# Both streams' h side by side in one tile, their shared products 512 columns wide, and the gate logits kept in DRAM until the merge

## The chip, the cores and the metric

The kernel runs on one core of a Trainium2 chip. The metric is the device time of one execution in microseconds. Engines are named as in the profile: PE is TensorE's matmuls and PEld its weight loads, DVE the vector engine, ACT the scalar engine, POOL GpSimd, SP SyncE, which issues most of the DMAs.

## What is computed

One layer over a latent stream x (256 tokens) and a context stream ctx (256 tokens), D = 2048, all in float32. Both streams are modulated and projected; only the latent stream goes on to an output. Cut to what matters here:

```python
mod, mod_c = silu(c) @ w_mod + b_mod, silu(c_ctx) @ w_mod + b_mod
h  = modulate(rmsnorm(x,   norm_g[0]), sh_a,  sc_a)
hc = modulate(rmsnorm(ctx, norm_g[0]), csh_a, csc_a)
# p = h @ w_in, split into c_q, c_kv, k_r, hg_q, hg_ff, hg_fb, hg_i, hg_g, gate_logits (for h and for hc)
attn_l = block_attention(q_l, concat([k_c, k_l]), concat([v_c, v_l]))      # 8 heads, latent queries
hgo_c, s_f, s_b = hgrn2_bidirectional(*hg_c[:6], zero, zero)               # 8 heads, context first,
hgo_l, _, _     = hgrn2_bidirectional(*hg_l[:6], s_f, s_b)                 # then latent from its states
g = sigmoid(gate_logits_l)                                                 # (256, 2, 2048)
out_l = (g[0] * (attn_l @ w_br_mla) + g[1] * ((rmsnorm(hgo_l) * silu(hgate)) @ w_br_hgrn)) @ w_out
x = x + gt_a * rmsnorm(out_l, norm_g[1])
h = modulate(rmsnorm(x, norm_g[2]), sh_f, sc_f)
x = x + gt_f * rmsnorm(swiglu(h, w_ffn_in, w_ffn_out), norm_g[3])
```

## The kernel before

**Arithmetic.** Channels lie on the 128 partitions and tokens on the columns. Every float32 operand of a product is split into a rounded high part and the rest, weights as wH and wL (`split_w`, the cast on ACT at line 100, the subtraction on DVE at line 102), activations as a pair (aH, aL). A product is wH·aH + wH·aL + wL·aH. K = 2048 is 16 slices of 128, k = 0 to 15. `mm3` (lines 116 to 125) writes these three products for each of the streams that it is given, all 256 columns wide: six matmuls per k for both streams (H·aH and H·aL of the first, of the second, then L·aH of each), three for one. `mm_wide` (lines 127 to 130) does one stream in two matmuls: the pair [aH | aL] side by side, 512 columns, with wH, then 256 columns with wL; the two halves of the result are added later.

**Order.** The kernel is written in program order, and a scheduler sets each engine's order from that, from the buffers of the pools and from modelled times. The pools are wp (three each of raw, wH, wL), ap (16 each of hA, hB; 8 of hC), bp (two of 32 KB per partition, tag b16) and two of PSUM, pj and px, four banks each. Weights come as raw tiles of 1 MB on SP's queue (`load_w`); the weights of the first six blocks (wst, tile rw) come on POOL's queue.

**Stages.**
- Startup, 0 to 143 us. 32 weight tiles for the modulation pass through PE (pm, line 256). As soon as a group of one or two k is modulated, `make_h` (lines 191 to 199) makes h of both streams for them, on DVE (195), ACT (196) and DVE (197), into one tile hA (latent) and one hB (context), each [aH | aL]. `pre_mm` then adds this k to the first six projection blocks (NPRE = 6, PSUM tiles pre).
- Latents and heads, to 555 us. `project` (lines 326 to 334) does one block of 128 output channels: 16 k's of `mm3` into one PSUM bank ps, the latent stream in columns 0 to 255, the context stream in 256 to 511. Eight heads (`hgrn_head`) have five blocks each; value and both forget gates are for both streams, query and output gate for the latent stream alone. While PE does one head's blocks, DVE and ACT do the gate chains (the scans that make the decays), and PE takes in the small products of the head before: transposes pk of the keys kt (line 471, copied to ktn at 474), chunk products pc (479).
- Gates and attention, to 827 us. `gates` (569 to 581) makes the 32 blocks of gate logits with `mm_wide`, 16 k's each; ACT copies one half out of PSUM, DVE adds the other, into a tile sgt (128 x 512, for both branches of one j) that takes the slot of an hB. The tiles pe of the softmax come from the hB slots as well. Attention is written between the gate blocks; its pk at line 125 has three 512-column matmuls per k, psS at 656 has three of 512 columns with 64 rows.
- Merge, to 919 us (lines 705 to 723). For each j of 16, 48 matmuls psb (line 713); sigmoid of sgt on ACT (715), multiplication by psb on DVE (716), the sum m of both branches on POOL (718), then the split into mg, which takes the slot of an hA.
- Output projection (`project_tok`, pst, line 778), norm, feed-forward, to the end. It reuses hA and hB slots for the split weights of the last tiles, h2 and G, and `gate_rows` (736 to 750) makes the second norm's gate vectors.

Of the kernel before, what the change touches and what calls it, by code (L numbers as in the profile page):

```python
# [14 lines left out]
P = 128  # L15
T = 256
# [10 lines left out]
def block_kernel(  # L27
# [83 lines left out]

    def split_act(dst, src, heng=None):
        nc.scalar.copy(dst[:, 0, :], src)
        nc.vector.tensor_tensor(dst[:, 1, :], src, dst[:, 0, :].bitcast(F32), op=ALU.subtract)
# [57 lines left out]
    hs = [[None] * KD, [None] * KD]  # L172
# [18 lines left out]
    def make_h(k):  # L191
        for s, tag in ((0, "hA"), (1, "hB")):
            h = ap.tile([P, 2, T], F32R, tag=tag, name=tag)
# [5 lines left out]
            hs[s][k] = h  # L199
# [126 lines left out]
    def project(nb, streams):  # L326
# [239 lines left out]
    aT = bp.tile([P, NH, 2, T], F32R, tag="b16", name="aT")  # L566
    sgt = []

    def gates(b):

        if b % 2 == 0:
            sgt.append(ap.tile([P, 512], F32, tag="hB", name="sgt"))
# [3 lines left out]
        for k in range(KD):  # L576
            mm_wide(ps, w(k * P, P), hs[0][k], k == 0, k == KD - 1)
# [66 lines left out]
    def att_s(i, A):  # L644
# [4 lines left out]
        for qb in range(2):  # L649
# [10 lines left out]
            pe = ap.tile([P, 512], F32, tag="hB", name="pe")  # L660
# [44 lines left out]
    mg = []  # L705
    for j in range(KD):
        w = split_w(load_w(wbr[j]))
# [28 lines left out]
    def gate_rows(i, tag, bufs):  # L736
# [8 lines left out]
        tiles = []  # L745
        for c in range(4):
            g = ap.tile([P, 512], F32, tag=tag, name="gbc", bufs=bufs)
            nc.sync.dma_start(g, gdr[i, 4 * c:4 * c + 4].rearrange("k p -> (k p)").partition_broadcast(P))
            tiles.append(g)
        return tiles  # L750

    def project_tok(tiles, nk, src, first, last, lead=None):
# [6 lines left out]
        for q in range(nq):  # L759
            raw = load_w(tiles(q))  # L760
            if lead and q == nq - 1:
                ws.append(split_w(raw, step=512, tags=(lead[0], lead[0]), pool=ap, bufs=lead[1]))
# [31 lines left out]
    g1b = gate_rows(0, "hC", 8)  # L794
# [281 lines left out]
```

## Time and profile before

| | us |
|---|---|
| median of 3 runs | 1767.45 (1766.27 to 1767.64) |
| profiled execution | 1768.12 |
| its span in the trace | 1766.3 |
| PE busy | 1725.0 |
| DVE busy | 1110.0 |
| ACT busy | 800.1 |
| startup, to the last group's products | 0 to 143 |
| latents and heads | 143 to 555 |
| gates and attention | 555 to 827 |
| merge | 827 to 919 |

The rows of the trace follow after the change. Busy time counts the records of an engine; matmuls are pipelined and their records overlap, so what a matmul costs in a stream is read from the distance between starts. The chain that ended last is followed back from the last instruction, at each step to what released it. In rows on stretches of time the columns are: start and end of the stretch, its length, then for PE, PEld, DVE, ACT and POOL the busy us and in brackets the number of instructions, then the TensorE clock that was granted as a share of 2.4 GHz, the mean busy share of the 16 DMA engines, and GB/s. In timelines, "x4" is a run of four instructions, and brackets give the idle time before and what ended it.

### The profile page before, as it was taken

Reading aid. Unit: us, or ns where it says so; the run is one execution under the profiler, and the core shown is the slowest. Engines: PE = TensorE matmul, PEld = TensorE weight load, DVE = VectorE, ACT = ScalarE, POOL = GpSimd, SP = SyncE. Lnnn points to the kernel's source line nnn. Section 1 sums busy time; section 2 is a strip of 40 time slices with the busy share of each in tenths; the row PEclk is TensorE's granted clock in tenths of the full one; section 3 lists DMA queues with packets and bytes.
Section 4 is the critical chain, followed back from the end, with each engine's and each line's share of the span. In section 5 each row is a group of like instructions: output and inputs, shape, how many; then the busy total and the mean of one; then the engine's idle time right before and its main releaser. Section 6 shows DMA issues by size and latency. Waiting matters only on the chain.

```text
span 1766.3 us, 26819 instructions
## 1 busy us (share of the span) xinstructions
PE 1725.0 (98%) x10976; PEld 1528.4 (87%) x10976; DVE 1110.0 (63%) x1703; ACT 800.1 (45%) x1178; POOL 38.6 (2%) x57
## 2 busy tenths in 40 slices
PE   4999999999999999999999899999999999999998
PEld 2779999999999888888998698888888888888886
DVE  4335777766678766666775687776445555555556
ACT  4224433333334655555444554444444444334443
POOL 2100000000000000000110000000000000000000
PEclk9999999999999999999999999999999999999999
DMA  9985456555556555566765457777555555555563
GB/s 361 331 320 194 140 178 208 191 191 170 175 173 231 212 182 207 177 248 232 260 228 200 169 178 275 281 276 257 195 192 185 188 191 190 192 191 189 181 215 130
DMA packets 56459, 374.64 MB, mean 212 GB/s; under 512 B 6512, under 2 KB 6800, under 8 KB 13072
## 3 DMA queue, kind: packets, MB, share of 16 engines
q1 hardware_dynamic: 53424, 365.06, 59.1%
q0 software_dynamic: 2048, 6.29, 1.1%
q8 instruction: 86, 1.41, 0.3%
q10 hardware_dynamic: 864, 1.57, 0.2%
q14 instruction: 37, 0.30, 0.0%
HBM read 370.79 MB, written 2.11 MB: 211 GB/s over the span
## 4 chain that ended last, share of the span: by engine, by line
PE 97%; DVE 1%; DMA 1%; ACT 1%; issue 0%; SPq 0%; DVEq 0%; ACTq 0%
PE ps L125 20%; PE pst L778 18%; PE psf L129 18%; PE psf L130 9%; PE ps L129 7%; PE psb L713 5%; PE pre L125 4%; PE ps L130 3%; PE pm L256 2%; PE psf L872 1%; PE psS L656 1%; PE po L679 1%; PE psS L653 1%; DMA xt<-in_xT_dram 1%; PE pv L628 1%; PE pq L612 1%
## 5 line engine op out<-in xcount | busy, mean ns | idle before, releaser
L102 DVE TENSOR_TENSOR wL<-raw,wH 128x1024 fp32r<-128x1024 f32 (+1 forms) x492 | 597.5, 1217 | 462.4 <-ACT wH L100 461.3
L100 ACT CAST wH<-raw 128x1024 fp32r<-128x1024 f32 (+1 forms) x492 | 508.7, 1037 | 748.7 <-PE ps L125 182.1
L129 PE MATMUL psf<-h,wH 128*128 128x512 f32 x1344 | 475.1, 399 | 0.0
L130 PE MATMUL psf<-h,wL 128*128 128x256 f32 x1344 | 377.5, 281 | 0.0
L129 PEld LDWEIGHTS psf<-h,wH 128*128 128x128 f32 x1344 | 252.6, 188 | 62.8
L125 PE MATMUL ps<-hA,wH 128*128 128x256 f32 x1312 | 254.6, 285 | 0.0
L130 PEld LDWEIGHTS psf<-h,wL 128*128 128x128 f32 x1344 | 253.9, 189 | 0.2
L125 PEld LDWEIGHTS ps<-hA,wH 128*128 128x128 f32 x1312 | 204.8, 192 | 1.2 <-issue 0.5
L125 PE MATMUL ps<-hA,wL 128*128 128x256 f32 x656 | 187.3, 286 | 0.0
L129 PE MATMUL ps<-hA,wH 128*128 128x512 f32 x512 | 183.8, 400 | 0.0
L778 PE MATMUL pst<-wH,gA 128*128 128x512 f32 x576 | 166.6, 389 | 0.0
L321 DVE CUSTOM_DVE_ANT_0 raw<-raw,cb 128x2048 f32<-128x2048 f32 x64 | 146.0, 2281 | 29.9 <-DMA raw<-in_wm_dram 29.7
L130 PE MATMUL ps<-hA,wL 128*128 128x256 f32 x512 | 144.0, 282 | 0.0
L125 PE MATMUL ps<-hB,wH 128*128 128x256 f32 x672 | 137.2, 284 | 0.0
L778 PEld LDWEIGHTS pst<-wH,gA 128*128 128x128 f32 x576 | 108.0, 188 | 22.3
L125 PEld LDWEIGHTS ps<-hA,wL 128*128 128x128 f32 x656 | 125.7, 192 | 0.5 <-issue 0.5
L129 PEld LDWEIGHTS ps<-hA,wH 128*128 128x128 f32 x512 | 96.0, 188 | 22.9 <-issue 1.3
L125 PEld LDWEIGHTS ps<-hB,wH 128*128 128x128 f32 x672 | 105.0, 192 | 0.0
L778 PE MATMUL pst<-wL,gA 128*128 128x512 f32 x288 | 101.4, 389 | 0.0
L130 PEld LDWEIGHTS ps<-hA,wL 128*128 128x128 f32 x512 | 96.5, 189 | 2.6 <-DVE mx L658 1.1
L125 PE MATMUL ps<-hB,wL 128*128 128x256 f32 x336 | 95.2, 283 | 0.0
L778 PE MATMUL pst<-wH,mg 128*128 128x512 f32 x256 | 74.4, 389 | 0.0
(432 smaller groups left out, 2189.3 us busy)
## 6 DMA issues: line engine op xcount, KB each, us to landing
raw<-in_wm_dram SPq DMA_DIRECT2D x96, 1024.0 KB, 5.0
raw<-in_wfi_dram SPq DMA_DIRECT2D x84, 1024.0 KB, 4.9
raw<-in_win_dram SPq DMA_DIRECT2D x73, 1024.0 KB, 4.9
raw<-in_wfo_dram SPq DMA_DIRECT2D x44, 1024.0 KB, 4.8
raw<-in_wbr_dram SPq DMA_DIRECT2D x16, 1024.0 KB, 5.0
raw<-in_wout_dram SPq DMA_DIRECT2D x16, 1024.0 KB, 4.9
rw<-in_wst_dram POOLq DMA_DIRECT2D x16, 256.0 KB, 5.8
raw<-in_wqk_dram SPq DMA_DIRECT2D x4, 1024.0 KB, 4.9
```

The source lines that it names most:

```text
L100: nc.scalar.copy(H, raw[:, o:o + n])
L102: nc.vector.tensor_tensor(L, raw[:, o:o + n], H.bitcast(F32), op=ALU.subtract)
L125: nc.tensor.matmul(o, l, r, start=(first and i == 0), stop=(last and i == len(seq) - 1))
L129: nc.tensor.matmul(ps, w[0], act.rearrange("p e t -> p (e t)"), start=first, stop=False)
L130: nc.tensor.matmul(ps[:, 0:T], w[1], act[:, 0, :], start=False, stop=last)
L256: nc.tensor.matmul(pm[32 * (k % 4):32 * (k % 4) + 32, 0:n], cst[:, k], raw[:, kk * n:(kk + 1) * n], start=(k < 4), stop=(k >= KD - 4))
L321: nc.vector.tensor_tensor_reduce(out=raw, in0=raw, in1=cbt[0], scale=1.0, scalar=0.0, op0=ALU.mult, op1=ALU.add, accum_out=mod2[:, i // KD ...
L612: nc.tensor.matmul(pq[:, i * T:(i + 1) * T], l, r, start=(k == 0 and i == 0 and z == 0), stop=(k == 3 and i == 1 and z == 2))
L628: nc.tensor.matmul(pv[:, i, :], ckvs[:, k, l, ts_], r, start=(i == 0 and k == 0 and z == 0), stop=(i == 1 and k == 1 and z == 2))
L653: nc.tensor.matmul(psS, qn[a][:, i * T + qb * P:i * T + (qb + 1) * P], kn[b], start=(n == 0), stop=False)
L713: nc.tensor.matmul(ps[:, br * T:(br + 1) * T], l, r, start=(br == 0 and k == 0 and z == 0), stop=(br == 1 and k == NH - 1 and z == 2))
L778: mm = nc.tensor.matmul(ps[hf], l, r, start=(k == 0 and n == 0), stop=(k == nk - 1 and n == 2))
```

## The change

1. One tile hx in place of the 32 tiles hA and hB: partition x stream x k x part (high, low) x token. `both(k, 0)` is aH of both streams for one k, `both(k, 1)` is aL: two runs of 256 columns that lie apart in the tile. `pre_mm` and `project` give `mm3` one 512-column output for both streams, so that it writes three matmuls of 512 columns per k (now line 136) in place of six of 256. A block for one stream is as before.
2. Gate logits no longer stay on the chip: `gates` makes them in four places of a tile sgx (slots 0 to 3) and stores each j to DRAM (sgd, line 608); the merge loads them back (line 739) into eight places, four of which held the softmax's pe (slots 4 to 7). Both on POOL's queue. The sigmoid is now line 748, m is line 751.
3. Places in hx that have become free are given out by hand: the attention's output aT, the merged units mg, later h2 (`units`), the split weights of two tiles (`split_into`) and G (`spare`). The second norm's gate vectors go into the place of the modulation's operand (tag cst).

```diff
+    def split_into(raw, tiles):
+        for i, (H, L) in enumerate(tiles):
+            nc.scalar.copy(H, raw[:, i * 512:(i + 1) * 512])
+            nc.vector.tensor_tensor(L, raw[:, i * 512:(i + 1) * 512], H.bitcast(F32), op=ALU.subtract)
...
-    hs = [[None] * KD, [None] * KD]
+    hx = cp.tile([P, 2, KD, 2, T], F32R, name="hx")
+
+    def both(k, e):
+        return hx[:, :, k, e, :]
...
     def make_h(k):
-        for s, tag in ((0, "hA"), (1, "hB")):
-            h = ap.tile([P, 2, T], F32R, tag=tag, name=tag)
+        for s in range(2):
+            h = hx[:, s, k]
...
     def pre_mm(ws, k, b):
-        mm3([pre[b][:, 0:T], pre[b][:, T:2 * T]], ws(b * P, P),
-            [(hs[s][k][:, 0, :], hs[s][k][:, 1, :]) for s in range(2)], k == 0, k == KD - 1)
+        mm3([pre[b].rearrange("p (s t) -> p s t", s=2)], ws(b * P, P), [(both(k, 0), both(k, 1))],
+            k == 0, k == KD - 1)
...
-        outs = [ps[:, s * T:(s + 1) * T] for s in streams]
         for k in range(KD):
-            mm3(outs, w(k * P, P), [(hs[s][k][:, 0, :], hs[s][k][:, 1, :]) for s in streams], k == 0, k == KD - 1)
+            if len(streams) == 2:
+                o, act = ps.rearrange("p (s t) -> p s t", s=2), (both(k, 0), both(k, 1))
+            else:
+                o, act = ps[:, 0:T], (hx[:, 0, k, 0, :], hx[:, 0, k, 1, :])
+            mm3([o], w(k * P, P), [act], k == 0, k == KD - 1)
...
-    aT = bp.tile([P, NH, 2, T], F32R, tag="b16", name="aT")
-    sgt = []
+    aT = hx[:, 1, 0:NH]
+    sgx = bp.tile([P, 8, 512], F32, tag="b16", name="sgx")
+    sgd = dp.tile([KD, P, 512], F32, name="sgd")
+    n_pe = [0]
...
     def gates(b):
+        j = b // 2
...
-        half = sgt[-1][:, (b % 2) * T:(b % 2 + 1) * T]
+        half = sgx[:, j % 4, (b % 2) * T:(b % 2 + 1) * T]
         nc.scalar.copy(half, ps[:, 0:T])
         nc.vector.tensor_tensor(half, half, ps[:, T:2 * T], op=ALU.add)
+        if b % 2 == 1:
+            nc.gpsimd.dma_start(sgd[j], sgx[:, j % 4, :])
         step()
...
-            pe = ap.tile([P, 512], F32, tag="hB", name="pe")
+            pe = sgx[:, 4 + n_pe[0] % 4, :]
+            n_pe[0] += 1
...
+    units = [hx[:, 1, 8 + j] for j in range(8)] + [hx[:, 0, j] for j in range(8)]
+    spare = [hx[:, 1, j] for j in range(8)] + [hx[:, 0, 8 + j] for j in range(8)]
     for j in range(KD):
+        sg = sgx[:, (4 + j) % 8, :]
+        nc.gpsimd.dma_start(sg, sgd[j])
...
-        nc.scalar.activation(sgt[j], sgt[j], AF.Sigmoid)
-        nc.vector.tensor_tensor(sgt[j], ps, sgt[j], op=ALU.mult)
+        nc.scalar.activation(sg, sg, AF.Sigmoid)
+        nc.vector.tensor_tensor(sg, ps, sg, op=ALU.mult)
         m = wk.tile([P, T], F32, tag="hf", name="m", bufs=2)
-        nc.gpsimd.tensor_tensor(m, sgt[j][:, 0:T], sgt[j][:, T:2 * T], op=ALU.add)
-        dst = ap.tile([P, 2, T], F32R, tag="hA", name="mg")
+        nc.gpsimd.tensor_tensor(m, sg[:, 0:T], sg[:, T:2 * T], op=ALU.add)
+        dst = units[j]
...
-            h = ap.tile([P, 2, T], F32R, tag="hB", name="h2")
+            h = units[j]
...
-            g = ap.tile([P, 2, T], F32R, tag="hA", name="gA")
+            g = spare[n_g[0] % 16]
...
-            g2b = gate_rows(1, "hB", 16)
+            g2t = cp.tile([P, 4, 512], F32, tag="cst", name="g2t")
+            g2b = gate_rows(1, [g2t[:, c] for c in range(4)])
```

What this does to the engines' orders is shown at three places, the last of them (the handover of the gate logits) for two engines. A row is line, operation, output <- inputs, shape of the output and a count.

PE at the start of the first six blocks, before: pt and pm belong to the modulation, the pre tiles are the six blocks, hA is the latent stream's h of k = 0, and each block has H·aH first, then H·aL.

```order
L269 MATMUL pt<-c_84,row 128x2 x2
L125 MATMUL pre_95<-hA,wH 128x256
L125 MATMUL pre_96<-hA,wH 128x256
L125 MATMUL pre_97<-hA,wH 128x256
L125 MATMUL pre_98<-hA,wH 128x256
L125 MATMUL pre_95<-hA,wH 128x256
L125 MATMUL pre_96<-hA,wH 128x256
L125 MATMUL pre_97<-hA,wH 128x256
L125 MATMUL pre_98<-hA,wH 128x256
L256 MATMUL pm<-raw,cst 32x256 x16
```

The same place after the change, with ptok and pbc from the second stream's norm:

```order
L289 MATMUL pt<-c_84,row 128x2 x2
L276 MATMUL pm<-raw,cst 32x256 x16
L289 MATMUL pt<-c_84,row 128x2 x2
L154 MATMUL ptok<-ones,acc 128x1 x4
L166 MATMUL pbc<-dg,ones 128x128
L276 MATMUL pm<-raw,cst 32x512 x4
L166 MATMUL pbc<-dg,ones 128x128
L276 MATMUL pm<-raw,cst 32x512 x4
L136 MATMUL pre_96<-hx,wH 128x512
```

The first eight narrow products, which needed the latent stream alone, have left their place ahead of the sixteen pm; the first wide one stands behind the second stream's norm.

PE in the heads around the transposes pk of one pair of chunks, before:

```order
L125 MATMUL ps<-hA,wL 128x256
L125 MATMUL ps<-hB,wL 128x256
L125 MATMUL ps<-hA,wH 128x256 x2
L125 MATMUL ps<-hB,wH 128x256 x2
L471 MATMUL pk<-c_84,kt 128x128 x4
L479 MATMUL pc<-qd_2800,kt 128x128 x2
L125 MATMUL ps<-hA,wL 128x256
L125 MATMUL ps<-hB,wL 128x256
L125 MATMUL ps<-hA,wH 128x256 x2
L125 MATMUL ps<-hB,wH 128x256 x2
```

And after the change:

```order
L136 MATMUL ps<-hx,wH 128x512 x2
L136 MATMUL ps<-hx,wL 128x512
L136 MATMUL ps<-hx,wH 128x512
L494 MATMUL pk<-c_84,kt 128x128 x4
L502 MATMUL pc<-qd_2241,kt 128x128 x2
L136 MATMUL ps<-hx,wH 128x512
L136 MATMUL ps<-hx,wL 128x512
L136 MATMUL ps<-hx,wH 128x512 x2
L136 MATMUL ps<-hx,wL 128x512
```

Three wide rows stand where six narrow ones stood, and pk and pc come between the products as before.

POOL from the startup's last weight load on, before: the two memsets belong to the heads, m to the merge.

```order
L224 DMA rw<-in_wst_dram 128x512
L224 DMA rw<-in_wst_dram 128x256
L387 MEMSET hgx 128x512
L388 MEMSET hgx 128x1600
L718 ISA
L718 TENSOR_TENSOR m<-sgt 128x256 x16
```

And after the change:

```order
L410 MEMSET hgx 128x512
L411 MEMSET hgx 128x1600
L608 DMA sgd<-sgx 128x512 x13
L739 DMA sgx<-sgd 128x512 x3
L608 DMA sgd<-sgx 128x512
L739 DMA sgx<-sgd 128x512 x3
L608 DMA sgd<-sgx 128x512
L739 DMA sgx<-sgd 128x512
L608 DMA sgd<-sgx 128x512
L739 DMA sgx<-sgd 128x512
L751 ISA
L751 TENSOR_TENSOR m<-sgx 128x256
```

The merge's first eight loads have moved in between the last gate logits' stores, ahead of the first m, and from there on a load and an m alternate.

ACT where the sigmoids begin, before: L579 is the copy of a gate block, L715 the sigmoid, L474 belongs to the heads.

```order
L579 COPY sgt<-ps 128x256
L100 CAST wH<-raw 128x1024
L715 ACTIVATE sgt<-sgt 128x512
L474 COPY ktn<-pk 128x512
L100 CAST wH<-raw 128x512
L579 COPY sgt<-ps 128x256
L100 CAST wH<-raw 128x1024
```

And ACT at the handover from the gates to the merge, after the change: L605 is the copy of a gate block, L703 and L711 are attention, L124 is the high part of an activation, L748 the sigmoid of the logits that have come back.

```order
L605 COPY sgx<-ps 128x256
L703 COPY pT_7009<-pp 128x128 x2
L748 ACTIVATE sgx<-sgx 128x512
L703 COPY pT_7011<-pp 128x128 x2
L100 CAST wH<-raw 128x1024 x2
L605 COPY sgx<-ps 128x256
L748 ACTIVATE sgx<-sgx 128x512 x2
L711 COPY of<-po_7078 128x256
L124 CAST hx<-of 128x256
L100 CAST wH<-raw 128x1024 x2
L605 COPY sgx<-ps 128x256
L748 ACTIVATE sgx<-sgx 128x512
```

The sigmoids (L748) of j = 3, of j = 4 and 5 and of j = 6 stand between copies of the last three gate blocks and behind them, each with casts of weights behind it; those of j = 0 to 2 stand some rows higher. Before, the sigmoid of j = 0 followed on the copy of its own gate block, with no transfer between.

## Rows read from the trace of the kernel before

**Rows 1.** The page's busy time: us, share of the span and instructions per engine.
```profile
PE 1725.0 (98%) x10976; PEld 1528.4 (87%) x10976; DVE 1110.0 (63%) x1703; ACT 800.1 (45%) x1178; POOL 38.6 (2%) x57
```

**Rows 2.** The page's chain that ended last, by engine and by line.
```profile
PE 97%; DVE 1%; DMA 1%; ACT 1%; issue 0%; SPq 0%; DVEq 0%; ACTq 0%
PE ps L125 20%; PE pst L778 18%; PE psf L129 18%; PE psf L130 9%; PE ps L129 7%; PE psb L713 5%; PE pre L125 4%; PE ps L130 3%; PE pm L256 2%; PE psf L872 1%; PE psS L656 1%; PE po L679 1%; PE psS L653 1%; DMA xt<-in_xT_dram 1%; PE pv L628 1%; PE pq L612 1%
```

**Rows 3.** Stages: span, busy us (instructions) by engine, PEclk, DMA share, GB/s.
```profile
143.00:555.00 412.00, 412.00 (x3409) 409.89 (x3410) 292.58 (x581) 159.54 (x216) 1.90 (x2) 1.00 0.53 180
555.00:827.00 272.00, 272.00 (x1571) 232.13 (x1570) 185.17 (x297) 155.24 (x255) 0.00 (x0) 1.00 0.59 209
```

**Rows 4.** Waits, 143 to 555 us: engine, line, released by: us, times, longest.
```profile
ACT wH L100 <- PE ps L125: 182.1, 58, 5.6
```

**Rows 5.** Groups of PE by shape: xcount | busy us, mean ns | idle.
```profile
L125 PE MATMUL ps<-hB,wH 128*128 128x256 f32 x672 | 137.2, 284 | 0.0
...
L125 PE MATMUL ps<-hB,wL 128*128 128x256 f32 x336 | 95.2, 283 | 0.0
...
L125 PE MATMUL pre<-hB,wL 128*128 128x256 f32 x96 | 27.4, 286 | 0.0
```

**Rows 6.** Chain in order of time: start us, us, what.
```profile
277.64 21.35 PE ps L125 x178
...
328.97 21.35 PE ps L125 x178
...
717.50 0.90 PE psS L656 x3
...
1224.34 87.06 PE pst L778 x384
```

**Rows 7.** PE's timeline from 597 us: start us, us, what.
```profile
597.47 0.61 PE L125 MATMUL pk<-cqkv,wH 128*128 128x512 f32 x2
...
598.60 0.28 PE L130 MATMUL ps<-hA,wL 128*128 128x256 f32 x1
598.71 0.40 PE L129 MATMUL ps<-hA,wH 128*128 128x512 f32 x1
598.95 0.28 PE L130 MATMUL ps<-hA,wL 128*128 128x256 f32 x1
...
599.66 0.28 PE L130 MATMUL ps<-hA,wL 128*128 128x256 f32 x1
```

**Rows 8.** PE's timeline at three points of the startup; brackets: idle before.
```profile
28.07 1.22 PE L125 MATMUL pre<-hA,wH 128*128 128x256 f32 x4 [3.00 <-ACT hA L196]
...
86.15 1.43 PE L125 MATMUL pre<-hA,wH 128*128 128x256 f32 x7 [0.16 <-ACT hA L196]
...
143.00 1.62 PE L125 MATMUL pre<-hA,wH 128*128 128x256 f32 x7 [1.51 <-ACT hA L196]
```

**Rows 9.** The scalar engine's timeline at 85 us, the two streams' h.
```profile
85.59 0.51 ACT L196 ACTIVATE hA<-xt,SH 128x256 fp32r<-128x256 f32 x1 [1.52 <-DVE xt L195]
86.00 0.49 ACT L196 ACTIVATE hB<-xt,SH 128x256 fp32r<-128x256 f32 x1
```

**Rows 10.** Stretches of the startup, columns as in rows 3.
```profile
0.00:100.00 100.00, 75.67 (x560) 52.02 (x560) 40.40 (x109) 35.65 (x74) 17.72 (x37) 0.97 0.92 349
...
140.00:150.00 10.00, 8.49 (x59) 8.35 (x59) 3.62 (x11) 1.82 (x5) 1.90 (x2) 0.83 0.60 252
```

**Rows 11.** Tile rw: GpSimd's issues, ns min/median/max, and their landing.
```profile
L224 POOL DMA_DIRECT2D rw<-in_wst_dram x32: 536/538/686, 1.3 to 99.7; - x32
...
DMA to landing us min/median/max: 3.2/6.0/10.0
```

**Rows 12.** GpSimd's timeline in the merge.
```profile
840.59 1.65 POOL L718 TENSOR_TENSOR m<-sgt 128x256 f32<-128x256 f32 x1 [6.50 <-DVE sgt L716]
...
844.93 0.74 POOL L718 TENSOR_TENSOR m<-sgt 128x256 f32<-128x256 f32 x1 [2.69 <-DVE sgt L716]
```

**Rows 13.** DMA issues, 140 to 830 us: count, KB each, median us to landing.
```profile
raw<-in_wv_dram SPq DMA_DIRECT2D x4, 256.0 KB, 2.5
```

More of the change, by code (lines that the diff above doesn't have):

```diff
@@ L110, in split_w, with get @@
         return get
+    def split_into(raw, tiles):
+        for i, (H, L) in enumerate(tiles):
+            nc.scalar.copy(H, raw[:, i * 512:(i + 1) * 512])
+            nc.vector.tensor_tensor(L, raw[:, i * 512:(i + 1) * 512], H.bitcast(F32), op=ALU.subtract)
+        def get(o, n):
+            return tuple(t[:, o % 512:o % 512 + n] for t in tiles[o // 512])
+        return get
     def split_act(dst, src, heng=None):
@@ L170, in block_kernel, with wide @@
     SH1 = cp.tile([P, KD, 2], F32, name="SH1")
-    hs = [[None] * KD, [None] * KD]
+    hx = cp.tile([P, 2, KD, 2, T], F32R, name="hx")
+    def both(k, e):
+        return hx[:, :, k, e, :]
+    def wide(u):
+        return u.rearrange("p e t -> p (e t)")
     xs = []
@@ L198, in make_h @@
                                            op0=ALU.add, op1=ALU.subtract)
-            hs[s][k] = h
     NPRE = 6
@@ L744, in gate_rows @@
         nc.sync.dma_start(gdr[i], grow)
-        tiles = []
-        for c in range(4):
-            g = ap.tile([P, 512], F32, tag=tag, name="gbc", bufs=bufs)
+        for c, g in enumerate(tiles):
             nc.sync.dma_start(g, gdr[i, 4 * c:4 * c + 4].rearrange("k p -> (k p)").partition_broadcast(P))
-            tiles.append(g)
         return tiles
@@ L761, in project_tok @@
             if lead and q == nq - 1:
-                ws.append(split_w(raw, step=512, tags=(lead[0], lead[0]), pool=ap, bufs=lead[1]))
+                ws.append(split_into(raw, lead))
             else:
@@ L792, in rstd_part, with pairs @@
         return rt
-    g1b = gate_rows(0, "hC", 8)
+    def pairs(tiles):
+        return list(zip(tiles[0::2], tiles[1::2]))
+    g1b = gate_rows(0, [ap.tile([P, 512], F32, tag="hC", name="gbc", bufs=8) for _ in range(4)])
     x1 = bp.tile([P, 2, D], F32, tag="b16", name="x1")
@@ L802, in block_kernel @@
         cs = slice(c * 512, (c + 1) * 512)
-        ps = project_tok(lambda q: wout[c, q], KD, mg, True, True, ("hB", 16) if c == 3 else None)
+        ps = project_tok(lambda q: wout[c, q], KD, mg, True, True,
+                         pairs([wide(u) for u in spare[:8]]) if c == 3 else None)
         for hf in range(2):
@@ L811, in block_kernel @@
             sqrt_table(ssq[:, 0, 0, 0:1])
-    wfs0 = split_w(load_w(wfs[0]), step=512, tags=("hB", "hB"), pool=ap, bufs=16)
+    wfs0 = split_into(load_w(wfs[0]), pairs([wide(u) for u in spare[8:]]))
     xsc = [[None] * 4, [None] * 4]
@@ L858, in block_kernel @@
     G = [None] * NFF
+    n_g = [0]
     def ffn_first():
@@ L897, in swish @@
         else:
-            g = ap.tile([P, 2, T], F32R, tag="hA", name="gA")
+            g = spare[n_g[0] % 16]
+            n_g[0] += 1
         split_act(g, sa)
@@ L910, in ffn_out @@
             ps = project_tok(lambda q: wfo[c, q0 + q], 4 * nq, G[4 * q0:], part == 0, part == 2,
-                             ("hC", 8) if part == 2 and c == 3 else None)
+                             pairs([ap.tile([P, 512], F32R, tag="hC", name="wl", bufs=8) for _ in range(8)])
+                             if part == 2 and c == 3 else None)
             for hf in range(2):
```

5 lines of the change are left out of this document (2 added, 3 removed).

## The prediction

> **What bounds the kernel now.** I read the page's busy times first, then the chain that ended last. TensorE is busy for 1725.0 of 1766.3 us [rows 1] and makes up 97% of the chain [rows 2]; the reader is to see there that only TensorE's own stream sets the end, so that an edit is worth what it takes out of that stream, less what then has to be waited for. The chain also says where the stream is spent: ps at line 125, the projections in the heads, is its largest piece with 20%. The table by stage comes next [rows 3]: from 143 to 555 us, the eight heads, TensorE has work in every microsecond, while the vector engine is at 292.6 of 412 us and the scalar engine at 159.5. In that stage the scalar engine waits 182.1 us for TensorE to release weight buffers [rows 4]: the split weights lie ready ahead of their products. Last I read start times of single matmuls, since the records' durations overlap (a 256-column matmul is recorded with 284 ns [rows 5]) and only the distance between starts adds up to the span.
>
> **What a matmul costs by its width.** In an unbroken run in the heads 178 matmuls of 256 columns take 21.35 us, 119.9 ns each; in the output products 384 of 512 columns take 87.06 us, 226.7 ns each [rows 6]. Two narrow ones are 239.9 ns, so a wide one in their place saves 13.2 ns. The nearest form to the changed one, pk in the attention, has three 512-column matmuls per product with the weight order H, H, L: five of them start between 597.47 and 598.60 us, 226 ns each [rows 7]. I take 226.7. What no row shows is a moving operand in two runs of 256 columns that lie apart in memory, which is how the changed kernel reads both streams of one k; every row reads one run. Its bounds stand under the rivals.
>
> The Trainium skill, page "TensorE: Matmul & The Clock Gate", section "Wait — 56ns, not 53.3ns?", gives a fixed cost of about 2.5 ns per matmul beyond its columns. By it a merged pair would save 2.5 ns; rows 6 put 13.2 ns there, and the trace decides.
>
> **The change part by part.** (1) Heads and latents. A both-stream product is now 6 matmuls of 256 columns and will be 3 of 512. The records for the second stream count them: 672 with wH and 336 with wL [rows 5], so 336 products (21 blocks of 16) and 1008 pairs. 1008 x 13.16 ns = 13.3 us, all of it on the chain, since this stage has no free TensorE time [rows 3]. Blocks for the latent stream alone keep their three 256-column matmuls. What could take it back is the vector engine, whose load goes from 292.6 of 412 to 292.6 of 399 us, 73%: still not the bound, and the splits are ahead, so I count nothing back.
>
> (2) The first six blocks, done while the modulation weights stream in. 96 products [rows 5], 288 pairs, 288 x 13.16 = 3.8 us if all of it counts. Two things pull at it. The wide matmul needs both streams' h, so the eight matmuls of the first stream that now run from 28.07 us on (four stand in the row), in time in which TensorE would wait anyway [rows 8], lose that place: their 8 x 0.12 = 0.96 us of columns move into the full stretch. And each later group starts when the second stream's h is there: its step on the scalar engine starts at 86.00 instead of 85.59 us [rows 9], 0.41 us later in a group that waits. Against that, the seven matmuls from 86.15 us took 1.43 us [rows 8] where 6 x 0.12 + 0.28 = 1.00 would do: they stopped some 0.43 us for the low part, and six wide ones last 6 x 0.227 = 1.36 us, which covers that stop. So the second item is about nil. 3.8 - 0.96 = 2.8; I take 2.5, with 0 and 3.8 as ends. Zero would be a front bound by transfers: DMA is busy 0.92 of the first 100 us [rows 10].
>
> (3) The clock. In 140 to 150 us the granted clock is 0.83 of 2.4 GHz on the mean [rows 10], part of it at the lower level of 1.2 GHz, after TensorE had stood for 1.51 us [rows 8]; that is 1.7 us of lost clock. The wait in front of the last h stays, so I leave the clock as it is and put 1.7 us to either side in the range.
>
> (4) Gate logits through DRAM. 16 stores and 16 loads of 256 KB on GpSimd's queue. An issue takes 0.54 us there and at most 0.69 [rows 11]; GpSimd has nothing else until the merge, where one m, 0.7 to 1.7 us [rows 12], and one load stand against 48 x 0.12 = 5.76 us of products per j. 8 MB more beside a DMA share of 0.59 in 555 to 827 us [rows 3] is no burden. For j of 8 and up a load is issued eight iterations, 46 us, before its use. The tight place is the handover: the loads of j = 4 to 7 go to the places from which the logits of j = 12 to 15 are stored, so a last gate block, its store, a load and a sigmoid follow on each other, and the scalar engine has weight casts and evacuations of gate blocks queued behind that sigmoid, for which TensorE waits in turn. From the copy of such a gate block to the sigmoid that takes its place the new order has at least two more gate blocks, 2 x 16 x 0.353 = 11.3 us [rows 7], for j = 4 to 6; for j = 7 it has the first merged unit, 5.76 us of products and an m of up to 1.65, 7.4 us. The round trip is two issues and two landings: with the 2.5 us that a 256 KB load took in the attention stage [rows 13] 6.1 us, with the 6.0 us median of the crowded start [rows 11] 13.1 us. The stage is like the former, so: nothing, hidden by products; with the latter 1.8 us at each of three places and 5.7 at the fourth.
>
> (5) The sigmoids move from the attention stage into the handover and the merge, and 15 of 41 table loads on the scalar engine go. It is busy 155 of 272 us in the attention stage [rows 3] and off the chain: 0, and if it were not, a gain.
>
> (6) Fixed places for the merged units, the split weights, h2 and G: TensorE's order from the merge on is the same matmul for matmul: 0. The second gate vectors are fetched earlier, at the first output part of the feed-forward, on SyncE's queue, where a landing and four issues stand ahead of weight loads; each of those feeds 24 x 0.227 = 5.4 us of products and three buffers lie between: 0, at most 1 us.
>
> **The sum.** 13.3 + 2.5 = 15.8 us. The profiled execution took 1768.12 us, of which the span is 1766.3: 1752.3. It lies 0.67 us above the median of 1767.45, so the median goes to **1751.7 us**, 0.9% less.
>
> **Rivals.** (A) Width gives less. Where 512 and 256 columns alternate, three pairs take 1.06 us (598.60 to 599.66 [rows 7]), 353 ns a pair, so 233 ns for the wide one if the narrow one keeps 119.9: 6.5 ns saved, 1008 x 6.5 + 1.2 = 7.8 us, 1759.7. Against it: the changed stream does not alternate, and rows 6 are such a stream.
>
> (B) Width gives nothing: the wide matmul keeps the 0.24 us that it takes from start to start in that alternation (598.71 to 598.95 [rows 7]), just two narrow ones; 1767.4. The same row of five pk speaks against it. The Trainium skill's 2.5 ns, in the section named above, would give 1296 x 2.5 = 3.2 us and 1764.2, to a measurement nearly the same.
>
> (C) Slower: reading two runs costs. The dearest 512-column matmuls in the trace are those of psS with 64 rows, three in 0.90 us [rows 6], 300 ns. At that price each pair would lose 60 ns, 1296 x 60 = 78 us, 1845. It decides as soon as a wide matmul with two runs takes over 239.9 ns. For it speaks only that no row shows the form; against it that the distance between starts follows the columns in rows 6 and 7, with a small step per matmul.
>
> (D) The handover. With 3 x 1.8 + 5.7 = 11.1 us, 1762.8. For it: an in-order scalar queue with casts behind the sigmoid. Against it: gate products all around. The Trainium skill, page "SBUF — State Buffer", section "SBUF: two separate sides", says that GpSimd and a vector instruction lock each other out of a shared port, and that the descriptors of GpSimd's DMAs starve by it. The trace shows the lock on arithmetic (m takes 1.65 instead of 0.74 us [rows 12]), while an issue never took over 0.69 us [rows 11].
>
> (E) The change does not bring what it takes out: the heads' gate chains on the vector engine become late by what TensorE gains, 13.3 us come back as waits, 1765.0. Against it: 73% load.
>
> **How the numbers follow.** Forecast 0.78; A 0.05, B 0.03, C 0.04, D 0.06, E 0.04. A measurement of this kernel can tell about 0.2%, 3.5 us, from no change: forecast, A and D are faster, 0.89; B and E the same, 0.07; C slower, 0.04. The range: upward 2.5 for the front and 1.7 for the clock, and on to A and D, 1763; downward 1.3 for the front, 1.7 for the clock and 1 for gaps of which no row tells, 1747.5. It leaves out B, C and E, 0.11, and some tail.
>
> **What would show it.** Right: ps at line 136 starts every 227 ns in the heads; a head takes 1.9 us (144 x 13.2 ns) less than the 51.3 us from 277.64 to 328.97 [rows 6]; the front ends 2 to 3 us earlier; from the merge on all is as long as before. Wrong: starts 233 or 240 ns apart (A, B) or more (C); waits of TensorE on kt, ktn or wL in the heads (E); waits of the scalar engine for sgx at line 748, followed by waits of TensorE (D).

## The result: 0.3% slower, and what the profile after shows

| | us |
|---|---|
| before, median of 14 runs | 1767.07 (1765.98 to 1769.66) |
| after, median of 14 runs | 1772.28 (1768.21 to 1775.45) |
| ratio | 1.0031, 95% interval 1.0024 to 1.0038 |
| predicted | 1751.7 (1747.5 to 1763.0) |
| profiled execution after, its span | 1772.22, 1770.5 |

The forecast was 15.8 us less; 5 us more came out. The page of the kernel after, busy time and the chain by line (as rows 1 and 2 of before):

```profile
PE 1722.8 (97%) x9680; PEld 1457.5 (82%) x9680; DVE 1110.6 (63%) x1703; ACT 782.1 (44%) x1163; POOL 60.4 (3%) x89
...
PE ps L136 20%; PE pst L808 19%; PE psf L140 18%; PE psf L141 9%; PE ps L140 7%; PE psb L746 5%; PE pre L136 4%; PE ps L141 3%; PE psf L907 1%; PE pm L276 1%; DMA raw<-in_wm_dram 1%; PE psS L684 1%; PE po L708 1%; PE psS L681 1%; DMA xt<-in_xT_dram 1%; PE pv L656 1%
```

The chain is TensorE's as before, and its stream has 1296 matmuls less, yet its busy time fell by only 2.2 us. By stretch (columns as in [rows 3]):

```profile
143.00:555.00 412.00, 409.30 (x2389) 358.25 (x2390) 297.19 (x586) 160.96 (x218) 1.90 (x2) 1.00 0.52 182
555.00:827.00 272.00, 272.00 (x1572) 232.04 (x1571) 184.38 (x293) 132.52 (x232) 12.18 (x23) 1.00 0.64 233
```

TensorE, which had work in every microsecond from 143 to 555 us, is now idle for 2.7 us of them. And the chain in order of time (start us, us, what; as [rows 6]):

```profile
279.10 22.79 PE ps L136 x121
...
329.50 22.79 PE ps L136 x121
...
1222.34 89.97 PE pst L808 x384
```

A head takes 50.40 us (279.10 to 329.50) where it took 51.33; 1.9 less were forecast. The surprise is the last row: the output products pst, untouched by the change, matmul for matmul the same, take 89.97 us for 384, 234.3 ns each, where [rows 6] have 87.06 and 226.7.

All of the span by stage, from the start of each stage's first product in both traces; the third column is an experiment told below (hx at distance 0):

| stage | before | after | distance 0 | change | forecast |
|---|---|---|---|---|---|
| startup | 153.29 | 153.19 | 155.02 | -0.1 | -2.5 |
| latents, heads, gates, attention | 673.34 | 670.49 | 665.03 | -2.85 | -13.3 |
| merge | 92.24 | 92.13 | 92.24 | -0.1 | 0 |
| pst, four stretches | 325.68 | 334.85 | 325.69 | +9.17 | 0 |
| norm and psf | 512.86 | 508.46 | 512.10 | -4.40 | 0 |
| behind the start of the last product | 8.85 | 11.32 | 11.31 | +2.47 | 0 |
| span | 1766.25 | 1770.45 | 1761.39 | +4.2 | -15.8 |

So four things are to be explained: matmuls in stages that nobody touched have other times; the wide ones give less than they should; TensorE waits in the latents; and the end got longer.

### The profile page after: what moved, and what is told of

It reads as the page before. It is cut to its first block, busy times and chain, and to the rows that moved or that the text cites. A ratio compares the mean times of both kernels' runs of the same rounds, so it can differ in the third digit from the quotient of the medians.

```text
span 1770.5 us, 24284 instructions
## 1 busy us (share of the span) xinstructions
PE 1722.8 (97%) x9680; PEld 1457.5 (82%) x9680; DVE 1110.6 (63%) x1703; ACT 782.1 (44%) x1163; POOL 60.4 (3%) x89
## 4 chain that ended last, share of the span: by engine, by line
PE 96%; DMA 2%; DVE 1%; ACT 1%; issue 0%; SPq 0%; DVEq 0%; ACTq 0%
PE ps L136 20%; PE pst L808 19%; PE psf L140 18%; PE psf L141 9%; PE ps L140 7%; PE psb L746 5%; PE pre L136 4%; PE ps L141 3%; PE psf L907 1%; PE pm L276 1%; DMA raw<-in_wm_dram 1%; PE psS L684 1%; PE po L708 1%; PE psS L681 1%; DMA xt<-in_xT_dram 1%; PE pv L656 1%
## 5 line engine op out<-in xcount | busy, mean ns | idle before, releaser
L102 DVE TENSOR_TENSOR wL<-raw,wH 128x1024 fp32r<-128x1024 f32 x480 | 587.4, 1226 | 461.5 <-ACT wH L100 459.3
L100 ACT CAST wH<-raw 128x1024 fp32r<-128x1024 f32 x480 | 501.5, 1046 | 739.0 <-PE ps L136 194.8
L140 PE MATMUL psf<-hx,wH 128*128 128x512 f32 x1344 | 470.8, 393 | 0.0
L141 PE MATMUL psf<-hx,wL 128*128 128x256 f32 x1344 | 374.9, 279 | 0.0
L136 PE MATMUL ps<-hx,wH 128*128 128x512 f32 (+1 forms) x1312 | 334.2, 343 | 1.3 <-ACT lat L372 1.3
L140 PEld LDWEIGHTS psf<-hx,wH 128*128 128x128 f32 x1344 | 251.8, 187 | 60.0
L141 PEld LDWEIGHTS psf<-hx,wL 128*128 128x128 f32 x1344 | 251.8, 187 | 0.3
L136 PEld LDWEIGHTS ps<-hx,wH 128*128 128x128 f32 x1312 | 225.1, 188 | 31.2 <-ACT lat L372 1.5
L808 PE MATMUL pst<-wH,hx 128*128 128x512 f32 x800 | 237.2, 396 | 0.0
L136 PE MATMUL ps<-hx,wL 128*128 128x512 f32 (+1 forms) x656 | 224.8, 343 | 1.2 <-DVE wL L102 1.2
L140 PEld LDWEIGHTS ps<-hx,wH 128*128 128x128 f32 x512 | 96.0, 188 | 23.1 <-issue 1.7
```

Source lines behind the costliest of these rows:

```text
L100: nc.scalar.copy(H, raw[:, o:o + n])
L102: nc.vector.tensor_tensor(L, raw[:, o:o + n], H.bitcast(F32), op=ALU.subtract)
L136: nc.tensor.matmul(o, l, r, start=(first and i == 0), stop=(last and i == len(seq) - 1))
L140: nc.tensor.matmul(ps, w[0], act.rearrange("p e t -> p (e t)"), start=first, stop=False)
L141: nc.tensor.matmul(ps[:, 0:T], w[1], act[:, 0, :], start=False, stop=last)
L808: mm = nc.tensor.matmul(ps[hf], l, r, start=(k == 0 and n == 0), stop=(k == nk - 1 and n == 2))
```

## The experiments

**Start addresses, first try.** In the built program hx begins at byte 30560 of each partition, 32 past a multiple of 64; the operands of the other large products begin at multiples of 64. (It stands in the pool of the constants, behind a row of small tiles.) pst from hC, which is such a tile, kept its 227 ns from start to start in the trace after, and pst from hx did not. Theory 1 was that the two operands of a matmul must agree within 64 bytes. Three kernels test it (each pad is also set to zero once, which the cuts here and below leave out):

```diff
# align_hx, on the changed kernel
+    pad0 = cp.tile([P, 8], F32, name="pad0")
     hx = cp.tile([P, 2, KD, 2, T], F32R, name="hx")
+    pad1 = cp.tile([P, 56], F32, name="pad1")
# shift_rest, on the changed kernel
     hx = cp.tile([P, 2, KD, 2, T], F32R, name="hx")
+    pad1 = cp.tile([P, 8], F32, name="pad1")
# mis_before, on the kernel before, first in their pools
+    pad0 = ap.tile([P, 8], F32, name="pad0", bufs=1)
+    pad1 = bp.tile([P, 8], F32, name="pad1", bufs=1)
```

> The changed kernel with 32 bytes put ahead of hx in each partition and 224 behind it, so that hx begins at a multiple of 64 bytes like all other operands of the matmuls (it begins 32 bytes past one), and everything behind it keeps its place within 64 bytes. Theory 1 (start address): a matmul of 512 columns is slower by some 7 to 9 ns where its moving and its stationary operand do not start at the same place within 64 bytes. Then pst goes from 234 back to 227 ns from start to start, the wide products of the heads from 236 to 227, the narrow ones there from 122 to 120, the pair of psf from 350 to 353: some 9 + 9 + 2 + 2 - 4 = 18 us less, about 1754 us. Theory 2 (two runs, or the place of hx low in the memory): nothing of this changes, 1772 us, pst 234.

Measured 1770.06 us, ratio to before 1.0016 (1.0006 to 1.0026).

> The changed kernel with hx left where it is and 32 bytes put behind it, so that weights, hC and the other tiles behind hx also start 32 bytes past a multiple of 64. Theory 1 in its relative form (the two operands of one matmul must agree within 64 bytes): as fast as with hx moved, about 1754 us, pst at 227 ns. Theory 1 in its absolute form (each operand off 64 bytes costs): 1772 us or more, pst at 234 ns or more. Theory 2 (place of hx, two runs): 1772 us.

Measured 1764.45, 0.9988 (0.9978 to 0.9997).

> The kernel before with 32 bytes put ahead of the pool of hA, hB and hC and 32 ahead of the pool behind it; nothing else is changed. Theory 1: h, the merged units and G then start 32 bytes off the weights within 64. pst goes from 227 to 234 ns (1440 of them, about +10 us), the pair of psf from 353 to 350 ns (1340, -4 us), narrow products of the heads from 120 to 121 or 122 ns (3600, +3 to +6 us): 1776 to 1780 us. Theory 2: no change, 1767 us.

Measured 1752.52, 0.9918 (0.9903 to 0.9933): 32 bytes of nothing make the kernel before 14.5 us faster. Its pst did what was expected, as its chain shows:

```profile
1209.76 89.60 PE pst L782 x384
```

89.60 us for 384 are 233.3 ns. But its narrow products got cheaper, here the run of 178 in a head that took 21.35 us in [rows 6]:

```profile
275.04 20.77 PE ps L129 x178
```

That is 116.7 ns each where it was 119.9, and the pairs of psf went from 353.4 to 346.8 ns, together more than pst lost. Theory 1 falls: align_hx, with agreement within 64, has pst at 232.4 ns, and shift_rest at 233.3. What stays is that the place of operands sets the time of a matmul, and that theory 2 (two runs) explains none of this.

**Products alone.** Two kernels leave out the layer and run TensorE on products with nothing beside them, one execution of each. H and L say which part of the weights a matmul uses; H, H, L is the order of `mm3` for one stream.

> Products alone, without the layer: runs of 24 matmuls H, H, L of 512 columns (ob to oi), runs of 16 pairs 512 and 256 (oj to oq), runs of 24 with a moving operand in two runs of 256 (or to ot), runs of 24 with 256 columns (ou to ox), each with other offsets of the moving and the stationary operand (moving, stationary, in bytes: 0 0; 32 0; 32 32; 0 32; 16 0; 64 0; 8 0; 48 0 / 0 0; 32 0; 16 0; 8 0; 4 0; 64 0; 48 0; 32 32 / 0 0; 32 0; 32 32 / 0 0; 32 0; 16 0; 64 0), then 0 0 of the first two kinds again. Theory 1: 227 ns where both agree within 64 bytes (0 0; 32 32; 64 0) and 231 to 238 where they differ; pairs 353 at 0 0 and 350 at 32 0; two runs cost no more than one. Theory 2: no offset makes a difference, and two runs take 234 ns against 227. If neither shows, the cause needs the rest of the kernel's traffic.

PE's timeline of it (start us, us of a run of matmuls, engine, line, out<-in):

```profile
19.81 5.78 PE L71 MATMUL ob<-X,W 128*128 128x512 f32 x24
25.65 5.86 PE L71 MATMUL oc<-X,W 128*128 128x512 f32 x24
31.57 5.75 PE L71 MATMUL od<-X,W 128*128 128x512 f32 x24
...
114.33 5.72 PE L71 MATMUL or<-X,W 128*128 128x512 f32 x24
120.11 5.86 PE L71 MATMUL os<-X,W 128*128 128x512 f32 x24
126.03 5.75 PE L71 MATMUL ot<-X,W 128*128 128x512 f32 x24
```

ob, oc, od have the offsets 0 0, 32 0, 32 32 (moving, stationary): the time of the run goes up with one offset and back with both, so the distance between the operands counts, not either's place. or, os, ot are the same three with two runs of 256 columns: not dearer (5.72, 5.86, 5.75). Rival C's price of two runs is nil. And og, at 64 0, settles at 229 ns: theory 1 is refuted here too.

> Products alone, without the layer, all distances of the moving from the stationary operand from 0 to 480 bytes in steps of 32: first 24 matmuls H, H, L of 512 columns each (aa is the start, ab at 0, ac at 32, to aq at 480), then pairs of 512 and 256 columns (ar at 0 to bg at 480), then H, H, L of 256 columns (bh at 0 to bw at 480). Theory 3: each pattern has its own time as a function of the distance, and the kernel's stages stand at the value of their distance: 512 columns 226.8 at 0, about 233 at 32, 235 at 96 or at 416 and 480, 229 to 232 at 64, 232 to 234 at 128 and 384; pairs 353.4 at 0, 347 at 32, 350 at 96; 256 columns 120 at 0, 117 to 119 at 32, 122 at 96, 115 to 118 at 64. Theory 2 has no dependence on the distance.

```profile
20.08 5.78 PE L71 MATMUL oab<-X,W 128*128 128x512 f32 x24
25.92 5.86 PE L71 MATMUL oac<-X,W 128*128 128x512 f32 x24
...
67.30 5.77 PE L71 MATMUL oaj<-X,W 128*128 128x512 f32 x24
73.12 5.86 PE L71 MATMUL oak<-X,W 128*128 128x512 f32 x24
...
114.51 5.92 PE L71 MATMUL oar<-X,W 128*128 128x512 f32 x32
120.49 5.82 PE L71 MATMUL oas<-X,W 128*128 128x512 f32 x32
...
209.43 3.14 PE L71 MATMUL obh<-X,W 128*128 128x256 f32 x24
212.63 3.07 PE L71 MATMUL obi<-X,W 128*128 128x256 f32 x24
...
228.44 2.99 PE L71 MATMUL obn<-X,W 128*128 128x256 f32 x24
```

oab and oac are H, H, L of 512 columns at 0 and 32, oaj and oak the same at 256 and 288: the pattern repeats after 256 bytes. oar and oas are pairs at 0 and 32: here 32 is the faster. obh, obi, obn are 256 columns at 0, 32 and 192. A run's sum holds some ten matmuls until the rhythm settles; settled, the starts are these ns apart (mean of the last twelve; pairs: of one pair):

| distance, bytes within 256 | 0 | 32 | 64 | 96 | 128 | 160 | 192 | 224 |
|---|---|---|---|---|---|---|---|---|
| H, H, L of 512 columns | 226.7 | 233.3 | 228.9 | 233.3 | 232.8 | 234.2 | 233.3 | 233.3 |
| pair of 512 and 256 | 353.3 | 346.7 | 348.8 | 350.0 | 351.2 | 346.7 | 353.3 | 353.3 |
| H, H, L of 256 columns | 120.0 | 116.7 | 117.8 | 120.0 | 120.0 | 117.5 | 113.3 | 118.2 |

The kernels stand on this table. Before, the distance is 0 in pst, psf and the merge: 226.8, 353.4 and 120. After, h2 is at 96 (psf 350.1) and pst, whose moving operand is the weight, at 160 (234.2). align_hx has 128 (psf 351.2, pst 232.4), mis_before 32 and 224 (346.8, 233.3). Theory 3, distance within 256, holds in these stages within half a ns a matmul. The wide products of the latents and heads follow it too, within some 1 ns, though they are often interrupted: 233.4 ns from start to start at 96 (after), 232.4 at 128 (align_hx), 229.7 at 64 (shift_rest).

The distance alone does not fix the time, though. shift_rest has all its pairs of psf at 64, where the table has 348.8; in its first stretch they stand at 353.3 ns, in the two later ones at 348.9, with instructions of the same shapes (psf alone, columns as in [rows 3] without POOL):

```profile
1060.00:1180.00 120.00, 120.00 (x681) 104.45 (x680) 8.71 (x21) 7.99 (x22) 1.00 0.76 283
1320.00:1440.00 120.00, 120.00 (x690) 105.10 (x689) 9.14 (x22) 7.66 (x21) 1.00 0.53 191
```

So one distance can have two settled rhythms. The half of mis_before's merge that reads aT is such a case as well: at 64 it takes 114.8 ns, where the table has 117.8 and shift_rest 118.2. What picks the rhythm is open.

**Distance 0, and the width alone.** Pads of 40 and 24 floats in place of 8 and 56 put hx at distance 0.

> The changed kernel with 160 bytes put ahead of hx and 96 behind it, so that hx and the weight tiles start at the same place within 512 bytes (distance 0; as changed it was 96, in the two runs with smaller shifts 384 and 64). Theory 3 (distance): the time from start to start of a matmul goes by the distance of its moving from its stationary operand within 512 bytes, in a way that differs by pattern; at distance 0 it is 226.8 ns for H, H, L of 512 columns, 353.4 for a pair of 512 and 256, 120 for 256 columns. Then pst takes 9.0 us less than as changed, the wide products of the heads 8.9, those of the startup 1.8, narrow ones about 1, and psf and the gates 5 more: 1756.6 us. Theory 2 (two runs in one moving operand, or its place low in the memory): the wide products of the heads stay at 235 ns, and at most pst changes: 1763 us or more.

Measured 1761.46 us, 0.9969 (0.9957 to 0.998), 10.8 below the changed kernel where theory 3 wanted 15.7. Its chain:

```profile
279.64 22.35 PE ps L136 x121
...
329.30 22.35 PE ps L136 x121
...
1217.01 87.08 PE pst L812 x384
```

pst is back at 226.8 ns, and a head takes 49.66 us. The stage table has the rest: latents to attention 5.5 us less than as changed, pst 9.2 less, norm and psf 3.6 more; its startup happened to be 1.8 us longer.

```diff
# narrow_512, on the kernel with distance 0, in project; pre_mm likewise
...
-            mm3([o], w(k * P, P), [act], k == 0, k == KD - 1)
+            mm3([ps[:, s * T:(s + 1) * T] for s in streams], w(k * P, P),
+                [(hx[:, s, k, 0, :], hx[:, s, k, 1, :]) for s in streams], k == 0, k == KD - 1)
```

> The kernel with distance 0, but with the both-stream products written as before, six matmuls of 256 columns per k on hx: the width alone is undone. Theory 3: 1296 pairs at 2 x 120 in place of 226.8 ns, 13.2 ns each, 17 us more than with distance 0: 1772 to 1774 us, of which the heads have 13.3. Theory 2: two runs cost what the width saves, and this one is no slower than its wide twin.

Measured 1769.78, 8.3 us above its wide twin; theory 3 wanted 17. A head in it takes 51.33 us, as before, so the 1.67 us per head are the width's, 11.6 of 13.2 ns for each of 144 pairs. It has no wait in the latents, while its wide twin has, so not all of the 11.7 us of seven heads reach the end. Its startup ends at 152.3 us; those of the wide kernels of this study end between 150.1 and 155.0: the width gives nothing there that shows.

**The end.** The gate logits' DMAs go to another queue.

```diff
# align_sp, on the kernel with distance 0
-            nc.gpsimd.dma_start(sgd[j], sgx[:, j % 4, :])
+            nc.sync.dma_start(sgd[j], sgx[:, j % 4, :])
...
-        nc.gpsimd.dma_start(sg, sgd[j])
+        nc.sync.dma_start(sg, sgd[j])
```

> The kernel with distance 0, and the gate logits' stores and loads issued by SyncE in place of GpSimd. Theory T (tail): the last drain of GpSimd, 7.08 us in the trace after and 4.47 before, lasts by the number of DMAs that GpSimd issued (64 against 32) and holds back the end by 2.4 us; with 32 issues left it takes 4.5 us again, and this kernel is 2.4 us below the one with distance 0, some 1754 us, unless SyncE's waits for a store delay weight loads. Rival: the drain waits for something else of the changed end (the place of the gate vectors), then the end stays 11.3 us behind the last product.

Measured 1759.52, 0.995 (0.9933 to 0.9968), 1.9 us below align_512 in the medians. From the last vector instruction to the end of the trace it takes 3.08 us as before, with GpSimd's last long drain (an instruction of that name, with which its stream ends) at 4.47 us; align_512 has 5.54 and 7.09. Theory T holds. The merge took 0.7 us longer, with SyncE's queue shared.

**Choosing distances.** If theory 3 is right, the kernel before can be made faster without any of the change.

```diff
# before_192, on the kernel before, first in its pool
+    pad0 = ap.tile([P, 48], F32, name="pad0", bufs=1)
# before_mix: the same, first in the pool behind, and between hA and hB
+    pad2 = bp.tile([P, 8], F32, name="pad2", bufs=1)
...
+                padded.append(ap.tile([P, 56], F32, name="pad1", bufs=1))
# wide_mix, on the changed kernel, beside the SyncE issues and a pad of 48 ahead of hC
-                h = units[j]
+                h = off160(24 + j, 40) if j < 8 else off160(j - 8, -24)
```

(off160(i, o) is place i of hx, o floats further on.)

> The kernel before with 192 bytes put ahead of the pool of hA, hB and hC; nothing else is changed, so activations stand 192 bytes off the weights within 256, narrow products stay narrow. Theory 3 (distance): 256 columns at 113.3 in place of 120 ns, some 3500 of them up to the gates, 23 us, and 766 in the merge, 5 us; pst at 228.9 in place of 226.7, 3 us more; psf and gates at 353.3 as before. Less 4 us of waits in the latents and heads, as TensorE gets ahead of the splits there, and a few us until the rhythm settles behind each break: 1743 to 1750 us. Theory 1 (agreement within 64 bytes): as before, since 192 is a multiple of 64: 1767 us. If width were what counts: 1767 us.

Measured 1755.12, 0.9929 (0.9911 to 0.9947). That is 5 us above the range expected. The merge did as expected, 114.3 ns and 4.4 us less, and pst 228.9. The heads did not; their run of 178:

```profile
272.44 20.97 PE ps L127 x178
```

It has 117.8 ns a matmul in place of 113.3. The order there is H, H, H, H, L, L, which the table does not have; it has H, H, L, which is the merge's. That the order makes the difference is argued, not tested: at 32 the same order in mis_before had the table's 116.7.

> As the run with 192 bytes, but with hB (the context stream's h, later h2 of the feed-forward) at a distance of 160. Theory 3: the pairs of psf at 346.7 in place of 353.3 ns, 1343 of them, 8.9 us less; the second stream's narrow products at up to 117.5 in place of 113.3, 1296 of them, at most 5.4 us more, and the two distances in turn may disturb each other: 2 to 9 us below the run with 192 bytes.

Measured 1748.81, 0.9898 (0.988 to 0.9916): 6.3 us less than before_192: psf has 346.8 ns a pair and takes 10.1 us less than before, while the heads take 1.2 more than in before_192.

> The changed kernel with wide products and each place chosen by its distance: hx at 0 for the wide products and for pst, h2 moved within hx to 160, hC and cqkv at 192, the gate logits' DMAs on SyncE. Theory 3: against the kernel with distance 0 and SyncE (1759.5), psf takes 10.1 us less (as in the run with hB at 160), the half of psb that reads hC 2.2, the query products 1, pst with hC some 0.4 more: 1746 to 1748 us, at or a little below the narrow kernel with chosen distances (1748.8). If width were worth its 13.3 us beside the distances, it would have to come out at 1740 or less.

Measured 1745.49, 0.988 (0.9864 to 0.9897). At the distances chosen for each, the wide kernel is 3.3 us below the narrow one in the medians, and 1.7 us if each is taken against the kernel before that ran beside it (20.3 and 18.7 us less). The intervals of the two ratios overlap: whether the wide kernel is faster at all is not shown here, but it is not by 13.3 us. It still has its waits in the latents, which the narrow one has not.

**The waits in the latents.** In the kernel after (engine, line waited for: us, times, longest):

```profile
PE ps L136 <- ACT lat L372: 1.3, 1, 1.3
PE ps L136 <- DVE wL L102: 1.2, 1, 1.2
```

The scalar engine's and the vector engine's timelines after, at 158 us:

```profile
158.50 1.28 ACT L328 ACT_TABLE_LOAD   x1
159.79 1.92 ACT L328 ACTIVATE cbs<-cb 128x2048 f32<-128x2048 f32 x1
161.73 1.28 ACT L145 ACT_TABLE_LOAD   x1
163.02 0.69 ACT L145 ACTIVATE ktn<-ss,epst 128x512 f32<-128x512 f32 x1
```

```profile
161.74 2.29 DVE L329 TENSOR_TENSOR cb<-cb,cbs 128x2048 f32<-128x2048 f32 x1 [2.00 <-ACT cbs L328]
163.95 3.35 DVE L146 RECIPROCAL ktn<-ktn 128x512 f32<-128x512 f32 x1
167.21 3.43 DVE L102 TENSOR_TENSOR wL<-raw,wH 128x1024 fp32r<-128x1024 f32 x3
```

And before, the same two:

```profile
158.74 0.69 ACT L134 ACTIVATE ktn<-ss,epst 128x512 f32<-128x512 f32 x1 [0.17 <-PE ss L352]
159.44 1.28 ACT L308 ACT_TABLE_LOAD   x1
160.74 1.92 ACT L308 ACTIVATE cbs<-cb 128x2048 f32<-128x2048 f32 x1
```

```profile
159.74 3.35 DVE L135 RECIPROCAL ktn<-ktn 128x512 f32<-128x512 f32 x1
163.00 2.23 DVE L309 TENSOR_TENSOR cb<-cb,cbs 128x2048 f32<-128x2048 f32 x1
165.15 1.21 DVE L102 TENSOR_TENSOR wL<-raw,wH 128x1024 fp32r<-128x1024 f32 x1
```

Before, the square root of the latents' norm (ktn) stood ahead of cbs, the sigmoid for the later modulation; now the scheduler puts cbs and its table load ahead, ktn comes 4.3 us later, the reciprocal behind it too, and the next split wL at 167.21 in place of 165.15. The last kernel writes that sigmoid behind the first head:

```diff
-    make_cb()
...
         hgrn_head(h)
+        if h == 0:
+            make_cb()
```

> The wide kernel with chosen distances (1745.5), with one step written later: the sigmoid that prepares the vector of the later modulation (cbs, with its table load) is written behind the first head, so that the scheduler no longer puts it ahead of the latents' rstd on the scalar engine. Theory W (waits): as changed, that order puts the rstd, the reciprocal behind it and the splits of weights behind that 2 to 4 us later than before, and TensorE waits twice in the latents, 2.5 us together; now those waits are gone and the time is 1743 us. Rival: TensorE is simply ahead of the splits by what the wide products save, the waits stay or move on, and the time stays at 1745.5.

Measured 1743.81, 0.9874 (0.9856 to 0.9891). The difference of 1.7 us in the medians is within their spread, but the trace is clear. Its vector engine has the reciprocal and the next split early again:

```profile
159.49 3.35 DVE L148 RECIPROCAL ktn<-ktn 128x512 f32<-128x512 f32 x1 [1.19 <-ACT ktn L147]
162.76 1.16 DVE L104 TENSOR_TENSOR wL<-raw,wH 128x1024 fp32r<-128x1024 f32 x1
```

TensorE no longer waits there, and from the first product of the latents to the first of the gates it takes 386.49 us where wide_mix has 389.55. Theory W holds. This is the fastest kernel of the study, 22.7 us below the kernel before that ran beside it.

## Why the prediction was wrong, by its own steps

- **What a matmul costs by its width** is the step that failed. It took 226.7 and 119.9 ns [rows 6] as prices of a width, where they are prices at distance 0, at which all the large products of the kernel before happened to stand. The table has 226.7 to 234.2 and 113.3 to 120.0: two narrow matmuls at their best distance cost what a wide one costs at its best. [rows 7] held a warning: a pair in alternation takes 353 ns, not 226.7 + 119.9 = 346.6, so that 13.2 ns was no fixed step. It was used for rival A and dropped, since the changed stream does not alternate. A head gave 0.93 us for its 144 pairs as changed, 6.5 ns a pair, and 1.67 us at distance 0, 11.6 ns, not 13.2; a wide matmul in it took 237.0 and 231.8 ns on the mean, interruptions included. That rival A had 6.5 ns too is luck, since its reason was another. The Trainium skill, page "TensorE: Matmul & The Clock Gate", section "Wait — 56ns, not 53.3ns?", has about 2.5 ns fixed. The table does not agree: beyond its columns at 2.4 GHz (106.7 and 213.3 ns) a matmul took 6.6 to 20.9 ns here.
- **(1) Heads, -13.3.** -2.85 came with attention. 5.5 of the gap are the distance of 96 (align_512), 3.1 the waits (wide_cb), and the rest, some 2, is left at distance 0 (0.23 us a head). Starts of a settled rhythm are 226.7 ns apart there, the second to tenth behind a break 224 to 236; that this is the rest is argued from the starts, not tested.
- **The splits are ahead, so I count nothing back.** Wrong by those 3.1 us. It was read from sums over 143 to 555 us, most of which are the heads; the latents ahead of them are tighter, and the order of the scalar engine there was not compared.
- **(2) The first six blocks, -2.5.** 0, the lower end; that transfers bound it, the prediction's reading of [rows 10], was not tested. The startup ended at 150.1 to 155.0 us in the wide kernels of this study and at 151.3 to 153.3 in the narrow ones, in no relation to width.
- **(3) The clock.** It was left alone, rightly: 0.993 over both spans, and 0.83 in 140 to 150 us of both.
- **(4) Gate logits through DRAM.** The handover costs TensorE nothing, as forecast, although the landings were nearer to the startup's than to the attention's (issues, KB each, us to landing):

```profile
sgd<-sgx POOLq DMA_DIRECT2D x16, 256.0 KB, 5.8
sgx<-sgd POOLq DMA_DIRECT2D x16, 256.0 KB, 5.2
```

  The first of rival D's two signs came, waits of the scalar engine for sgx (780 to 925 us: us, times, longest):

```profile
ACT sgx L748 <- DMA sgx<-sgd: 9.3, 5, 3.5
```

  The second, waits of TensorE behind them, did not: TensorE waited for nothing in that window. From the start of the last gate product to that of the first of the merge it is 0.12 us in both traces, and the merge took 92.1. What the step missed is the price at the other end of the kernel: 32 more issues on GpSimd lengthen its last long drain by 2.61 us, and the end by 2.47.
- **(5)** The sigmoids cost nothing: right.
- **(6) From the merge on the same matmul for matmul: 0.** The premise was right and the conclusion wrong: +9.2 in pst, -4.4 in norm and psf. At distance 0 pst is back at its time before, and norm and psf within 0.8 us of theirs: the place of the operands did it.
- **Rivals.** C, the slower one, had the right sign, at 0.04, and the wrong mechanism: two runs cost nothing. E came in part, as waits of 3 us. No rival was about where operands lie, though the change moves nearly all of them.

## What to carry to other kernels

A change that moves operands changes the times of matmuls that it does not touch: look at the starts of an untouched stage first, and compare addresses of the moving and the stationary operand within 256 bytes as closely as instructions. A pad of 8 to 56 floats is a cheap trial, and here (14.5 us for mis_before, 18.7 for before_mix) it was worth more than the merge of matmuls (8.3 us, narrow_512 against align_512). Measure a form's price at the place at which it will stand, and in its order: each pattern in the table has its own best distance.

## What the runs showed of the hardware

- The start-to-start time of an fp32r matmul goes by the distance in bytes between its moving and its stationary operand, with a period of 256 in steps of 32 from 0 to 480 and a rhythm that repeats every few matmuls, with no other engine at work (micro2): up to 3% for 512 columns, 6% for 256. The Trainium skill, page "SBUF — State Buffer", section "Who interferes with whom", gives TensorE two independent read ports, one for the moving operand and one for weights. In these runs a matmul's time goes by how far apart the two operands lie, so for these matmuls the two reads are not independent in time. Where they meet, in the memory or behind it, is open.
- One distance can have two settled times: pairs of 512 and 256 columns at 64 took 353.3 and 348.9 ns in two stretches of shift_rest.
- A moving operand in two runs of 256 columns, 16 KB apart, costs what one run of 512 does (226.7 ns, micro), and so it does in hx at distance 0, where the runs lie 32 KB apart (226.7 once settled, align_512).
- GpSimd's last long drain takes 4.47 us with 32 DMAs issued on its queue in the startup (before, align_sp) and 7.08 with 32 more in the attention and the merge (after): an estimate of 82 ns for each of these. The kernel then ends 5.55 us behind the last vector instruction in place of 3.08.
